# A hybrid decoder layer on one core: marking norm, attention, eviction and residual chains as going ahead in the queues

## The chip, the cores and the metric

One core of one Trainium2 chip runs the whole layer in one launch. The metric is device time in microseconds, from runs of the compiled kernel; the median of three is given, and one more execution is profiled.

## The reference, cut to what matters

Sequence 256, width 2048, all float32. A conditioning vector c gives shift, scale and gate of both halves of the layer.

```
mod = silu(c) @ w_ada + b_ada
sh1, sc1, g1, sh2, sc2, g2 = split(mod, 6)
h = rmsnorm(x, norm1_g) * (1 + sc1) + sh1
q_sb, k_sb, v_sb, q_ds, k_ds, v_ds, q_ix, k_ix, w_ix = split(h @ w_in)
# 8 heads of 128
o_sb = stick_breaking_attention(q_sb, k_sb, v_sb)
# rotary on q_ds, k_ds, q_ix, k_ix; an indexer picks 64 keys per query; 8 heads share k, v
o_ds = dsa_attention(q_ds, k_ds, v_ds, q_ix, k_ix, w_ix * idx_scale)
merged = concat(rmsnorm(o_sb, sb_norm_g), rmsnorm(o_ds, dsa_norm_g))
x = x + g1 * (merged @ w_out)
h2 = rmsnorm(x, norm2_g) * (1 + sc2) + sh2
# up to 2 x 5504, causal depthwise convolution of width 3, silu gate, down
x = x + g2 * conv_ffn(h2, w_up, conv_w, conv_b, w_down)
return rmsnorm(x, final_norm_g)
```

## The kernel before, in words

Activations lie transposed (features on partitions, 256 tokens along the row). Every weight is loaded as 1 MB into one of four `raw` buffers by SP's queue (`load`, L135). `split` (L142) makes a high part with a cast on ACT (`wh`) and the remainder with a subtraction on DVE (`wl`), 1024 columns at a time, four buffers of each. A float32 product is then three matmuls: high by high, low by high, high by low (`nat`, `trn`, `fold`).

The stages, in the order in which they are written:

- The input projection in two parts of eight row blocks each (`do_A`, `do_A2`, `do_V`, `do_QK`); `put` (L346) evicts an accumulator, the second time adding to what is there.
- The sparse-attention group (L518 to L660) for the second part's results: rotary (`rope`), indexer scores `rel`, eight rounds of a maximum per query on DVE, a softmax attention per half of the tokens, and its norm: `rms_b` with the name `rds`, then `norm_o(od)`, which gives `odh` and `odl`. It is written ahead of `do_V` and `do_QK` of the second part (L698 to L701), which PE can do beside it.
- Eight stick-breaking heads, each `do_QK(h)` and then `sb_head(h)`: score `z`, four steps on ACT and one on DVE, a matmul `u` for the running sums, an exponential, the product `o`, and a sum of squares into `sqs` (a part of `ws`; L696).
- The output projection. It has eight blocks m, each with a first half for the sparse heads, `do_O(m, 0)`, and a second half for the stick-breaking heads, `do_O(m, 1)`. Four accumulators exist, so four first halves (L718 to L721) can run before any second half. Behind these in the text stand `rms_b([sqs])` with the name `rsb` (L724) and `norm_o(os_)` (L727), which gives `osh` and `osl`; then the second halves, each followed by `resid` for two of the sixteen row blocks.
- The second norm (`r2`, L762), `modulate` for the feed-forward input (`h2_make`), the up projection with convolution and gate (`do_U`, L835 on), the down projection (L871 on) and the last norm.

The conditioning products are spread over all of this: `ada(j)` (L223) loads 1 MB of `w_ada` and makes one column of `mod` with one DVE product (`wa`, L225); `ada_pe` (L194) makes four on PE (`ap`, `aq`). `pump()` writes a few of them at each call, as many as the string `PLAN` says.

What sets the order in the queues: each instruction gets a number in the order in which it is written. Before the run, a planner goes through the program with a model of the engines. Whenever an engine is free in that model, it queues there the ready instruction with the lowest number. An instruction is ready when its inputs are done and a buffer for its output is free. On the chip each engine then follows its queue in that order. `order(...)` adds single constraints by hand, among others for the first splits of the up projection (L807 to L810).

Of the kernel before, what the change touches and what calls it, by code (L numbers as in the profile page):

```python
# [54 lines left out]
def layer(ctx: ExitStack, tc: tile.TileContext, a, out):  # L55
# [12 lines left out]
    def sm(n, name):  # L68
        return wp.tile([P, n], F32, name=name, tag="sm", bufs=8)

    psum_pool = [None]

    def ps(name, dt=F32, tag="ps"):
# [32 lines left out]
    def rb(name):  # L106
        return wp.tile([P, S], F32, name=name, tag="rb", bufs=2)

    def rms_b(sqs_, width, y, name, tag):


        pt = ps(name + "p", tag=tag)
        for t in range(NT):
            for i, sq in enumerate(sqs_):
                T.matmul(pt[:, t:t + 1], lhsT=sq[:, t * P:(t + 1) * P], rhs=nones[:, 0:1], start=i == 0,
                         stop=i == len(sqs_) - 1)
        nss = pt[:, 0:NT]
        l = sm(NT, name + "l")
        A.activation(l, nss, AF.Ln, scale=-1.0 / width, bias=epsc)
        v = sm(NT, name + "v")  # L120
        V.tensor_scalar(out=v, in0=nss, scalar1=-1.0 / width, scalar2=EPS, op0=ALU.mult, op1=ALU.add)
        r = sm(NT, name + "y")
        A.activation(r, l, AF.Exp, scale=-0.5)
        V.scalar_tensor_tensor(out=l, in0=r, scalar=-0.5, in1=r, op0=ALU.mult, op1=ALU.mult)
        V.tensor_tensor(out=l, in0=l, in1=v, op=ALU.mult)
        last = V.scalar_tensor_tensor(out=r, in0=l, scalar=1.5, in1=r, op0=ALU.add, op1=ALU.mult)
        pt = ps(name + "b", tag=tag)
        for t in range(NT):
            T.transpose(pt[:, t * P:(t + 1) * P], r[:, t:t + 1].to_broadcast([P, P]), ident)
        if y is None:  # L130
            return pt[:, 0:S]
        A.copy(out=y, in_=pt[:, 0:S])
        return last, pt[:, 0:S]
# [145 lines left out]
    for g in range(4):  # L279
        pt = ps(f"cb{g}")  # L280
        for j in range(4):
            k = 4 * g + j
# [9 lines left out]
    V.scalar_tensor_tensor(out=b1, in0=par[:, PB + 16:PB + 32], scalar=1.0, in1=par[:, PN1:PN1 + KT], op0=ALU.add,  # L292
                           op1=ALU.mult)

    def rope(x, t, H, rd, o, name):

        h = rd // 2
        u = s2([P, H, rd], F32, name + "u")
        v = s2([P, H, rd], F32, name + "v")
        c = rc[:, t:t + 1, o:o + rd].to_broadcast([P, H, rd])  # L300
        V.tensor_tensor(out=u, in0=x, in1=c, op=ALU.mult)
        s0 = rs[:, t:t + 1, o:o + h].to_broadcast([P, H, h])
        s1 = rs[:, t:t + 1, o + h:o + rd].to_broadcast([P, H, h])
        V.tensor_tensor(out=v[:, :, 0:h], in0=x[:, :, h:rd], in1=s0, op=ALU.mult)
        V.tensor_tensor(out=v[:, :, h:rd], in0=x[:, :, 0:h], in1=s1, op=ALU.mult)
        V.tensor_tensor(out=x, in0=u, in1=v, op=ALU.add)
# [36 lines left out]
    vsb = b8([P, NT, 1024], F32, "vsb")  # L343
    qk = [b8([P, 8, S], F32, f"qk{i}") for i in range(2)]

    def put(half, dst, src, scale=1.0):  # L346
        if half == 0:
            if scale == 1.0:
                A.copy(out=dst, in_=src)
            else:  # L350
                A.mul(out=dst, in_=src, mul=scale)
        elif scale == 1.0:
            V.tensor_tensor(out=dst, in0=src, in1=dst, op=ALU.add)
        else:
            V.scalar_tensor_tensor(out=dst, in0=src, scalar=scale, in1=dst, op0=ALU.mult, op1=ALU.add)
# [159 lines left out]
    ptag[0] = "acc"  # L515


    for t in range(NT):  # L518
        rope(a2[:, t, 0:ID].rearrange("p (h d) -> p h d", h=1)[:, :, 0:16], t, 1, 16, 32, f"ki{t}")
        rope(qix[:, t, :].rearrange("p (h d) -> p h d", d=ID)[:, :, 0:16], t, IH, 16, 32, f"qi{t}")  # L520
# [15 lines left out]
            A.copy(out=qixT[:, 4 * g:4 * g + 4, t * P:(t + 1) * P], in_=pt.rearrange("p (k t) -> p k t", k=4))  # L536

    sc_n = [0]
    pump()

    def sc_t(L, name):
        sc_n[0] += 1
# [3 lines left out]
    for t in range(NT):  # L546
        L = P * (t + 1)
        cmt = cm[:, P:S] if t == 0 else cm
        npb = 512 // L
        sacc = [None, None]  # L550
        for g in range(8 // npb):
            pts = [ps(f"rel{t}{g}{par_}", tag="att") for par_ in range(2)]
            for j in range(npb):
                for par_ in range(2):
                    T.matmul(pts[par_][:, j * L:(j + 1) * L],  # L555
                             lhsT=qixT[par_ * ID:(par_ + 1) * ID, g * npb + j, t * P:(t + 1) * P],
                             rhs=kixT[par_ * ID:(par_ + 1) * ID, 0:L], start=True, stop=True)
            for par_ in range(2):
                rl = s2([P, npb, L], F32, f"rl{t}{g}{par_}")
                A.activation(rl, pts[par_].rearrange("p (n l) -> p n l", n=npb), AF.Relu)  # L560
                for j in range(npb):
                    h = (g * npb + j) * 2 + par_
                    if sacc[par_] is None:
                        sacc[par_] = sc_t(L, f"sacc{t}{par_}")
                        if par_ == 0:
                            V.scalar_tensor_tensor(out=sacc[0], in0=rl[:, j, :], scalar=wix[:, t, h:h + 1], in1=cmt,
                                                   op0=ALU.mult, op1=ALU.add)
                        else:
                            V.tensor_scalar(out=sacc[1], in0=rl[:, j, :], scalar1=wix[:, t, h:h + 1], scalar2=None,
                                            op0=ALU.mult)  # L570
                    else:
                        V.scalar_tensor_tensor(out=sacc[par_], in0=rl[:, j, :], scalar=wix[:, t, h:h + 1],
                                               in1=sacc[par_], op0=ALU.mult, op1=ALU.add)
        V.tensor_tensor(out=sacc[0], in0=sacc[0], in1=sacc[1], op=ALU.add)
        cur, nxt = sacc
        for r in range(8):
            m8 = sm(8, f"m8{t}{r}")
            V.max(out=m8, in_=cur)
            V.match_replace(out=nxt, in_to_replace=m8, in_values=cur, imm_value=-3e38)
            cur, nxt = nxt, cur  # L580
        mb[t] = scw[:, 6 + t, 0:L // 2].bitcast(BF16)
        V.tensor_scalar(out=mb[t], in0=cur, scalar1=-2e38, scalar2=NEG, op0=ALU.is_gt, op1=ALU.mult)
        V.tensor_tensor(out=mb[t], in0=mb[t], in1=cmt, op=ALU.add)
        pump()

    for t in range(NT):
        rope(a2[:, t, 80:80 + HD].rearrange("p (h d) -> p h d", h=1)[:, :, 0:32], t, 1, 32, 0, f"kx{t}")
# [15 lines left out]
    for t in range(NT):  # L603
# [29 lines left out]
        for g in range(2):  # L633
            pt = ps(f"av{t}{g}", tag="att")
            pv = pt.rearrange("p (k t) -> p k t", k=4)
            for s_ in range(t + 1):
                T.matmul(pv, lhsT=a2[:, s_, 80 + HD:80 + 2 * HD], rhs=pT[:, s_, 4 * g:4 * g + 4, :],
                         start=s_ == 0, stop=s_ == t)
            A.activation(dsq[:, 4 * g:4 * g + 4, t * P:(t + 1) * P], pv, AF.Square)
            for j in range(4):  # L640
                h = 4 * g + j
                A.activation(od[:, h, t * P:(t + 1) * P], pv[:, j, :], AF.Copy, scale=par[:, PDG + h:PDG + h + 1])
        pump()
    for w_ in (4, 2):
        V.tensor_tensor(out=dsq[:, 0:w_, :], in0=dsq[:, 0:w_, :], in1=dsq[:, w_:2 * w_, :], op=ALU.add)
    rdb = rb("rds")
# [1 line left out]
    odh = b8([P, NH, S], F32R, "odh")  # L648
    odl = b8([P, NH, S], F32R, "odl")

    def norm_o(o, rb_, oh, ol):
        for h in range(0, NH, 4):
            sl = slice(h, h + 4)
            V.tensor_tensor(out=o[:, sl, :], in0=o[:, sl, :],
                            in1=rb_.rearrange("p (n t) -> p n t", n=1).to_broadcast([P, 4, S]), op=ALU.mult)
            A.copy(out=oh[:, sl, :], in_=o[:, sl, :])
            V.tensor_tensor(out=ol[:, sl, :], in0=o[:, sl, :], in1=oh[:, sl, :].bitcast(F32), op=ALU.subtract)

    norm_o(od, rdb, odh, odl)
    pump()  # L660


    os_ = b8([P, NH, S], F32, "os")
    sbt = b8([P, D], F32, "sbt")

    def sb_head(h):
        q = qk[h // 4][:, (h % 4) * 2, :]
        k = qk[h // 4][:, (h % 4) * 2 + 1, :]
# [62 lines left out]
    x1T = [b8([P, 8, S], F32, f"x1T{i}") for i in range(2)]  # L731
    sq2 = ws[:, 1536:1792]

    def resid(dst, acc, gate, res, sqsum, k, name):

        resid_i[0] = V.scalar_tensor_tensor(out=dst, in0=acc, scalar=gate, in1=res, op0=ALU.mult, op1=ALU.add)  # L736
        if k == 0:
            A.activation(sqsum, dst, AF.Square)
            return None
        sq = s2([P, S], F32, f"{name}{k}")  # L740
        resid_i[1] = A.activation(sq, dst, AF.Square)  # L741
        if k >= KT - 2:
            return sq
        V.tensor_tensor(out=sqsum, in0=sqsum, in1=sq, op=ALU.add)

    for m in range(8):
# [6 lines left out]
        for p_ in range(2):  # L753
            k = 2 * m + p_
# [13 lines left out]
    def h2_make(k):  # L768
        if k in made:
# [4 lines left out]
        i, j = k // 8, k % 8  # L774
        am = amul[:, 16 + k:17 + k]
        sh = mod_cols(k, 64, 48, am, PN2, b2)
        modulate(h2[k // 4][:, k % 4, 0, :], h2[k // 4][:, k % 4, 1, :], x1T[i][:, j, :], am, r2p if k < 3 else r2, sh,
                 f"g2_{k}", False)

    for k in range(8):  # L780
# [187 lines left out]
```

## Time and profile before

| | us |
|---|---|
| median of 3 runs | 1222.13 (1219.72 to 1223.40) |
| the profiled execution | 1222.48 |
| its span, first to last instruction | 1220.70 |
| PE busy in it | 1154.4 (95%) |
| DVE busy | 879.5 (72%) |
| ACT busy | 632.2 (52%) |
| mean granted TensorE clock | 0.976 |
| read from HBM | 300.24 MB |

PE is TensorE's matmuls, PEld its weight loads, DVE is VectorE, ACT ScalarE, SP the engine that issues the loads. A busy PE isn't PE at its peak: its matmuls overlap, so the distance from one start to the next tells the pace. In a row of the timeline the bracket at the end is the idle time of the engine before that instruction and what ended it; "x4" means that four in a row were merged. A granted clock of 1.00 is 2.4 GHz and 0.50 is 1.2 GHz.

### The profile page before, as it was taken

How to read it: one execution, taken by the hardware profiler on the slowest of the kernel's cores; microseconds unless marked ns; L12 is line 12 of the kernel's file. 1: busy time of each engine (PE TensorE's matmuls, PEld its weight loads, DVE VectorE, ACT ScalarE, POOL GpSimd, SP SyncE). 2: the span in 40 equal slices, each digit the busy share in tenths (PEclk: the TensorE clock that was granted, in tenths of full speed). 3: DMA queues.
4: the chain of work that ended last, by engine and by line, in shares of the span. 5: the costliest groups of instructions: out<-in, count | busy, mean ns of one | idle time of the engine just before them, and what ended most of it. 6: DMA issues, size and time to landing. Idle time of an engine off the chain costs nothing.

```text
span 1220.7 us, 17725 instructions
## 1 busy us (share of the span) xinstructions
PE 1154.4 (95%) x7120; PEld 1018.6 (83%) x7120; DVE 879.5 (72%) x1267; ACT 632.2 (52%) x1004; POOL 0.2 (0%) x4
## 2 busy tenths in 40 slices
PE   3699999899999797999999999999999999999996
PEld 2578997668878797999888888888888888888885
DVE  4877787689766698878789787787876745454543
ACT  3356554457465344456565556555655644444441
POOL 0000000000000000000000000000000000000000
PEclk9799999899999898999999999999999999999998
DMA  8988899668788498776568666675665555555541
GB/s 308 391 318 333 330 324 335 256 222 329 260 341 331 141 346 306 246 275 238 177 246 336 241 210 225 222 254 208 246 224 202 178 198 183 196 184 189 191 139 69
DMA packets 43282, 303.48 MB, mean 249 GB/s; under 512 B 4928, under 2 KB 5440, under 8 KB 7232
## 3 DMA queue, kind: packets, MB, share of 16 engines
q1 hardware_dynamic: 43200, 302.35, 68.1%
q8 instruction: 55, 0.90, 0.3%
q14 instruction: 27, 0.22, 0.0%
HBM read 300.24 MB, written 2.10 MB: 248 GB/s over the span
## 4 chain that ended last, share of the span: by engine, by line
PE 89%; DVE 6%; ACT 3%; DMA 1%; issue 1%; SPq 0%; DVEq 0%; ACTq 0%
PE U L168 21%; PE W L168 13%; PE U L166 11%; PE W L166 7%; PE U L173 3%; PE U L174 3%; PE U L175 3%; PE O L174 3%; PE O L175 3%; PE QK L173 3%; PE QK L175 3%; PE O L173 3%; PE QK L174 3%; DVE wa L225 2%; PE ap L202 1%; PE A L151 1%
## 5 line engine op out<-in xcount | busy, mean ns | idle before, releaser
L225 DVE SCALAR_TENSOR_TENSOR wa<-wa,scb 128x2048 f32<-128x2048 f32 x76 | 173.2, 2284 | 3.8 <-DMA wa<-wa 3.5
L844 ACT COPY u<-U 128x256 f32<-128x256 f32 x70 | 26.1, 372 | 116.6 <-PE U L168 116.6
L845 DVE TENSOR_TENSOR u<-U,u 128x256 f32<-128x256 f32 x70 | 29.3, 420 | 58.7 <-ACT u L844 58.7
L855 DVE SCALAR_TENSOR_TENSOR uc<-u,par,uc 128x255 f32<-128x255 f32 (+1 forms) x140 | 63.8, 478 | 0.8
L851 ACT ACTIVATE uc<-u,par 128x256 f32<-128x256 f32 x70 | 41.9, 601 | 0.0
L862 ACT CAST aT<-uc 128x256 fp32r<-128x256 f32 x43 | 17.4, 404 | 33.3 <-DVE uc L861 33.3
L323 ACT ACTIVATE amul<-mod,b,par 128x1 f32<-128x1 f32 x32 | 12.1, 385 | 42.8 <-DVE wa L225 42.6
L890 DVE SCALAR_TENSOR_TENSOR x1T<-W,mod,x1T 128x256 f32<-128x256 f32 x16 | 7.7, 481 | 31.1 <-PE W L166 31.1
L741 ACT ACTIVATE x2q<-x1T 128x256 f32<-128x256 f32 x15 | 6.3, 418 | 39.1 <-DVE x1T L736 39.0
L326 ACT ACTIVATE mod<-mod,par 128x1 f32<-128x1 f32 x32 | 8.5, 294 | 30.5 <-DVE wa L225 29.4
L202 PE MATMUL ap<-wg,csil 128*32 128x512 f32 x160 | 23.5, 642 | 0.7 <-DMA wg<-wg 0.5
L857 ACT ACTIVATE uc<-uc 128x256 f32<-128x256 f32 x43 | 17.9, 416 | 7.7 <-DVE uc L855 7.6
L861 DVE TENSOR_TENSOR uc<-uc 128x256 f32<-128x256 f32 x43 | 18.2, 422 | 2.8
L863 DVE TENSOR_TENSOR aT<-uc,aT 128x256 fp32r<-128x256 f32 x43 | 18.0, 418 | 0.8 <-ACT aT L862 0.7
L855 DVE SCALAR_TENSOR_TENSOR uc<-U,par,uc 128x255 f32<-128x255 f32 (+1 forms) x32 | 15.0, 478 | 1.0 <-ACT uc L851 0.6
L686 ACT ACTIVATE sbt<-sbt 128x384 f32<-128x384 f32 x8 | 4.2, 525 | 20.6 <-DVE sbt L685 20.6
L202 PEld LDWEIGHTS ap<-wg,csil 128*32 128x32 f32 x160 | 4.3, 115 | 9.4 <-issue 7.0
L736 DVE SCALAR_TENSOR_TENSOR x1T<-O,mod,xT 128x256 f32<-128x256 f32 x16 | 7.0, 479 | 6.7 <-PE O L175 6.7
L555 PE MATMUL rel<-ws,qixT 64*128 64x128 f32 (+1 forms) x64 | 9.8, 390 | 1.5 <-ACT rl L560 1.5
L207 ACT COPY rw<-ap 128x512 f32<-128x512 f32 x5 | 2.9, 581 | 15.5 <-PE ap L202 15.5
L283 PE MATMUL cb<-ident,csil 128*128 128x128 f32 x16 | 3.6, 423 | 7.6 <-DMA ident<-ident 7.6
L151 PE MATMUL A<-wA00h,hh 128*128 128x512 f32 x4 | 2.5, 669 | 8.5 <-ACT hh L318 8.5
(2810 smaller groups left out, 4042.8 us busy)
## 6 DMA issues: line engine op xcount, KB each, us to landing
wU<-wU SPq DMA_DIRECT2D x86, 1024.0 KB, 4.8
wa<-wa SPq DMA_DIRECT2D x76, 1024.0 KB, 6.3
wD<-wD SPq DMA_DIRECT2D x43, 1024.0 KB, 4.8
wg<-wg SPq DMA_DIRECT2D x20, 1024.0 KB, 7.1
wA<-wA SPq DMA_DIRECT2D x16, 1024.0 KB, 6.7
wQK<-wQK SPq DMA_DIRECT2D x16, 1024.0 KB, 6.1
wO<-wO SPq DMA_DIRECT2D x16, 1024.0 KB, 5.7
xT<-xT SPq DMA_DIRECT2D x4, 512.0 KB, 6.0
```

The source lines that it names most:

```text
L166: T.matmul(pt[:, 1, :], lhsT=wl, rhs=x[:, 0, :], start=False, stop=stop)
L168: T.matmul(pt, lhsT=wh, rhs=x, start=first, stop=stop)
L173: T.matmul(pt, lhsT=wh, rhs=xh, start=first, stop=False)
L174: T.matmul(pt, lhsT=wh, rhs=xl, start=False, stop=False)
L175: T.matmul(pt, lhsT=wl, rhs=xh, start=False, stop=last)
L202: T.matmul(pt[32 * j:32 * j + 32, :], lhsT=csil[:, k:k + 1].to_broadcast([P, 32]), rhs=w[:, j * 512:(j + 1) * 512], start=q == 0, stop=q == 3)
L225: i = V.scalar_tensor_tensor(out=w, in0=w, scalar=1.0, in1=scb, op0=ALU.mult, op1=ALU.mult, accum_out=mod[:, j:j + 1])
L844: A.copy(out=u[:, gv, :], in_=acc[gv][:, 1, :])
L845: V.tensor_tensor(out=u[:, gv, :], in0=acc[gv][:, 0, :], in1=u[:, gv, :], op=ALU.add)
L851: A.activation(uc[:, gv, :], u[:, gv, :], AF.Identity, scale=par[:, PCW + 3 * i + 2:PCW + 3 * i + 3], bias=par[:, PCB + i:PCB + i + 1])
L855: V.scalar_tensor_tensor(out=uc[:, gv, sft:S], in0=u[:, gv, 0:S - sft], scalar=par[:, o:o + 1], in1=uc[:, gv, sft:S], op0=ALU.mult, op1=AL ...
L861: V.tensor_tensor(out=uc[:, 1, :], in0=uc[:, 0, :], in1=uc[:, 1, :], op=ALU.mult)
```

## The change

`tc.high_priority()` sets the number of what is written inside it back to the start of the program: the first instruction inside has number 0, the next 1. When it ends, the count goes on from where it had been. The change puts this around a set of chains, so their instructions have lower numbers than any other work that is ready at that moment. Each marked function, and each marked section, starts from 0 again, so marked chains stand among themselves by the place within their own function or section.

A decorator `ahead` marks whole functions: `rms_b` (all norms), `rope`, `put`, `sb_head`, `norm_o`, `resid`, and `modulate` where the second norm's result is applied. `begin()` and `end()` mark the sparse-attention group, left out around each `pump()`, so the conditioning products keep their numbers. Loads, splits and the projections' matmuls keep theirs too. No instruction is added or removed.

```
+    def ahead(f):
+
+        def g(*args, **kw):
+            with tc.high_priority():
+                return f(*args, **kw)
+        return g
+
+    guard = []
+
+    def begin():
+        guard.append(tc.high_priority())
+        guard[-1].__enter__()
+
+    def end():
+        guard.pop().__exit__(None, None, None)
...
+    @ahead
     def rms_b(sqs_, width, y, name, tag):
...
+    @ahead
     def rope(x, t, H, rd, o, name):
...
+    @ahead
     def put(half, dst, src, scale=1.0):
...
+    begin()
     for t in range(NT):
         rope(a2[:, t, 0:ID].rearrange("p (h d) -> p h d", h=1)[:, :, 0:16], t, 1, 16, 32, f"ki{t}")
...
     sc_n = [0]
+    end()
     pump()
+    begin()
...
         V.tensor_tensor(out=mb[t], in0=mb[t], in1=cmt, op=ALU.add)
+        end()
         pump()
+        begin()
...
                 A.activation(od[:, h, t * P:(t + 1) * P], pv[:, j, :], AF.Copy, scale=par[:, PDG + h:PDG + h + 1])
+        end()
         pump()
+        begin()
...
+    @ahead
     def norm_o(o, rb_, oh, ol):
...
     norm_o(od, rdb, odh, odl)
+    end()
     pump()
+    begin()
+    end()
...
+    @ahead
     def sb_head(h):
...
+    @ahead
     def resid(dst, acc, gate, res, sqsum, k, name):
...
-        modulate(h2[k // 4][:, k % 4, 0, :], h2[k // 4][:, k % 4, 1, :], x1T[i][:, j, :], am, r2p if k < 3 else r2, sh,
+        ahead(modulate)(h2[k // 4][:, k % 4, 0, :], h2[k // 4][:, k % 4, 1, :], x1T[i][:, j, :], am, r2p if k < 3 else r2, sh,
                  f"g2_{k}", False)
```

## Rows read from the trace of the kernel before

**Rows 1.** The page: the span, and each engine's busy time, share and instructions.

```profile
span 1220.7 us, 17725 instructions
PE 1154.4 (95%) x7120; PEld 1018.6 (83%) x7120; DVE 879.5 (72%) x1267; ACT 632.2 (52%) x1004; POOL 0.2 (0%) x4
```

**Rows 2.** Busy time by stretch; columns in the first row.

```profile
core 0: us, PE busy (x) PEld busy (x) DVE busy (x) ACT busy (x) POOL busy (x), PEclk, DMA share, GB/s
225.00:300.00 75.00, 70.28 (x397) 52.24 (x396) 66.28 (x162) 48.82 (x121) 0.00 (x0) 0.93 0.68 255
300.00:394.50 94.50, 91.13 (x675) 78.55 (x674) 66.25 (x87) 51.26 (x94) 0.00 (x0) 1.00 0.83 316
500.00:1200.00 700.00, 700.00 (x4239) 629.10 (x4238) 490.69 (x673) 374.89 (x533) 0.00 (x0) 1.00 0.61 215
...
375.00:394.70 19.70, 19.47 (x159) 19.15 (x159) 12.54 (x15) 10.31 (x18) 0.00 (x0) 1.00 0.94 359
394.70:412.00 17.30, 9.31 (x55) 8.53 (x55) 9.81 (x12) 5.24 (x8) 0.00 (x0) 0.70 0.34 134
412.00:475.00 63.00, 63.00 (x527) 63.00 (x527) 51.62 (x63) 29.43 (x43) 0.00 (x0) 1.00 0.81 299
...
398.20:408.40 10.20, 5.40 (x22) 4.71 (x23) 6.11 (x9) 2.85 (x4) 0.00 (x0) 0.50 0.50 202
```

**Rows 3.** Timeline of PE around the `rsb` norm: start, duration, instruction, idle before.

```profile
394.50 0.50 PE L115 MATMUL rsbp<-nones,ws 128*128 128x1 f32 x4
399.74 0.69 PE L129 MATMUL rsbb<-ident,rsby 128*128 128x128 f32 x2 [4.73 <-DVE rsby L126]
403.22 0.58 PE L173 MATMUL O<-osh,wO010h 128*128 128x256 f32 x1 [2.80 <-ACT osh L656]
...
411.84 0.28 PE L175 MATMUL O<-osh,wO011l 128*128 128x256 f32 x1
411.96 0.28 PE L174 MATMUL O<-osl,wO110h 128*128 128x256 f32 x1
```

**Rows 4.** Timeline of DVE in the same stretch.

```profile
382.16 0.42 DVE L696 TENSOR_TENSOR ws<-ws,sbt 128x256 f32<-128x256 f32 x1
384.14 1.23 DVE L146 TENSOR_TENSOR wO301l<-wO,wO301h 128x1024 fp32r<-128x1024 f32 x1 [1.56 <-ACT wO301h L145]
...
396.93 2.28 DVE L225 SCALAR_TENSOR_TENSOR wa<-wa,scb 128x2048 f32<-128x2048 f32 x1
```

**Rows 5.** Timeline of DVE and ACT around the twin norm, `rds`.

```profile
296.85 0.68 DVE L645 TENSOR_TENSOR dsq<-dsq 128x512 f32<-128x512 f32 x1
...
305.10 2.19 ACT L656 CAST odh<-od 128x1024 fp32r<-128x1024 f32 x2 [1.28 <-DVE od L654]
...
307.26 2.35 DVE L657 TENSOR_TENSOR odl<-od,odh 128x1024 fp32r<-128x1024 f32 x2
```

**Rows 6.** Timeline of ACT and DVE at the second norm, `r2`.

```profile
478.09 1.03 ACT L145 CAST wU101h<-wU 128x1024 fp32r<-128x1024 f32 x1
479.02 0.20 ACT L123 ACTIVATE r2y<-r2l 128x2 f32<-128x2 f32 x1
...
480.76 2.28 DVE L225 SCALAR_TENSOR_TENSOR wa<-wa,scb 128x2048 f32<-128x2048 f32 x1
```

**Rows 7.** Timeline of PE where the last head follows the one before.

```profile
371.35 0.38 PE L689 MATMUL o<-sbt,vsb 128*128 128x128 f32 x2
371.57 0.33 PE L671 MATMUL z<-sbm,identb 128*128 128x384 bf16 x1
```

**Rows 8.** Groups of DVE from 297 to 385: busy us, mean ns, idle before.

```profile
L225 DVE SCALAR_TENSOR_TENSOR wa<-wa,scb 128x2048 f32<-128x2048 f32 x8 | 18.3, 2282 | 0.4 <-DMA wa<-wa 0.4
L685 DVE TENSOR_TENSOR sbt<-u,sbt 128x384 f32<-128x384 f32 x8 | 4.4, 554 | 5.7 <-PE u L683 5.7
L680 DVE SCALAR_TENSOR_TENSOR sbt<-z,sbt 128x384 f32<-128x384 f32 x8 | 4.4, 553 | 4.6 <-ACT sbt L679 4.6
```

**Rows 9.** Waits of SP's queue: us in total, times, longest.

```profile
SPq L137 <- DVE wa L225: 155.5, 53, 7.3
```

## The prediction

> **What bounds the kernel now.** I read the page's busy shares first, then the stretches, then the order of time around each hole of PE. PE is busy for 1154.4 of 1220.7 us [rows 1]. From 500 to 1200 it is busy for 700.00 of 700.00 us at full clock [rows 2], so nothing that only reorders DVE or ACT there can gain, and the whole feed-forward part moves as one block behind whatever comes before it. The holes lie earlier. From 225 to 300 PE is idle for 4.7 us, from 300 to 394.5 for 3.4 us, and from 394.7 to 412 for 8.0 of 17.3 us, with a mean clock of 0.70 [rows 2]. That last stretch is the largest hole behind the start, and what ends it is one chain: the norm of the stick-breaking heads (`rsb`).
>
> The reader should see three times. The sum of squares that this norm needs is complete at 382.16 + 0.42 = 382.58 us [rows 4]. Its first matmul, `rsbp`, runs on PE only at 394.50 [rows 3], 11.9 us later, although its data are there. In between PE runs first halves of the output projection (`do_O(m, 0)` of L719), which are written ahead of L724 and therefore have the lower number. Then PE has nothing left that doesn't need `osh`, and it waits: 4.73 us for `rsbb`, 2.80 us for `osh` [rows 3]. The chain is in the wrong place by its number, not by its data.
>
> **The change part by part.** No instruction is added or removed; numbers are changed. I go by which other ready work a marked instruction overtakes: only work that is written earlier, since later work is already behind it.
>
> *The `rsb` norm and `norm_o(os_)`.* These overtake `do_O(0..3, 0)` and the `wa` products of L225 that are pumped before them. So `rsbp` goes to about 382.7 us, and its chain runs beside what is left of the first halves. Does it fit? The twin of this chain, `rds` with `norm_o(od)`, is written ahead of the projections that run beside it, so it shows what such a chain takes when nothing written earlier than it holds it up: its sum is complete at 296.85 + 0.68 = 297.53 us, its first `odh` cast begins at 305.10 (7.6 us later), its last `odl` ends at 307.26 + 2.35 = 309.61 (12.1 us later), with splits for the next weights among its steps [rows 5]. Put on 382.58 that gives `osh` from 390.2 and the last `osl` at 394.7, against 394.5 at which PE runs out of first halves today, plus about 1.2 us of `rsbp` and `rsbb` that now lie before that point (0.50 and 0.69) [rows 3]. It fits, narrowly, and the last `osl` isn't needed by the first matmuls. DVE has room: 12.54 us of 19.7 are busy from 375 to 394.7 [rows 2], and the chain brings two pairs of 2.4 us like the twin's and small change, some 5.5 us. A `wa` of 2.28 us that then comes later has no reader on this path.
>
> What that is worth: from 394.50 to 411.96 us PE does the 48 matmuls of `do_O(0, 1)`, one more, and the norm's own. At full clock one follows the other in 0.12 us [rows 3], so 49 are 5.9 us; with 1.2 us for the norm's it is 7.1 instead of 17.46 us. The gain is 10.4 us. Of this 7.5 us are the two waits; the other 2.9 are the third, short wait and matmuls at half clock: the granted clock is 0.50 (1.2 GHz) from 398.2 to 408.4 [rows 2], after PE had stood nearly still from 394.7, and without the hole I expect no fall.
>
> The Trainium skill (TensorE: Matmul & The Clock Gate, Terms) prices throttled time at its length times one less the granted share: 10.2 us at 0.50 would be 5.1 us on top of the waits, a time of about 1209.5. Half of this slow stretch is itself waiting, which a faster clock doesn't shorten, so the row decides. Nothing below rests on this paragraph.
>
> Can the rest follow 10.4 us earlier? From 394.7 to 475 the DMA engines bring 134 x 17.3 + 299 x 63 = 21.2 MB (GB/s times us, in thousandths); in 69.9 us that is 303 GB/s, and 359 is shown just before [rows 2]. DVE does 9.8 + 51.6 = 61.4 us in 80.3 us there; less the 5.5 that move ahead, 56 in 69.9. Both fit, so I carry the gain through whole.
>
> *The heads (`sb_head`, and `put` of their q and k).* These overtake `wa` and the PE form of it. Eight `wa` of 2.28 us stand among the heads' steps from 297 to 385 [rows 8]. But one head still follows the other: each `z` comes on PE directly behind the `o` of the head before (371.35, then 371.57) [rows 7], which I read as tiles of one kind being given out in written order, and a mark doesn't alter that. PE is busy for 91.13 of 94.5 us meanwhile [rows 2], so the gain is between 0 and 3.4 us. The loss is between 0 and 18.8 us, worked out under the third rival. I take 0: these heads are covered by projections, and PE's idle time there is already small.
>
> *The sparse-attention group (L518 to L660).* It is written ahead of the last value and query projections that fill PE, so it overtakes `wa`, `ap` and some of its own later parts, whose numbers now start again at each section. The gain is at most the 4.7 us of idle PE from 225 to 300; for the loss I set the same once more, as an estimate, because DVE is busy for 66.3 of 75 us there [rows 2] and any other order of its work is an order of the same work. I take 0.
>
> *The second norm (`r2`) and `modulate`.* Here the mark changes little. `r2y` of L123 is written before the weights of `do_U(1, 0)`, and yet the cast `wU101h` (478.09) goes ahead of it (479.02) [rows 6]. So the planner fills an idle engine with what is ready and doesn't hold it for a step that is about to be; a better number doesn't prevent that, nor the `wa` at 480.76 while `r2b` is on PE. Between 0 and 3.3 us (the 1.03 us cast and the 2.28 us `wa`) could be gained; I take 0. `resid` and the later `modulate` sit beside a full PE, and the first and last norms have little beside them: 0 both ways.
>
> **Sum.** The profiled execution took 1222.48 us (span 1220.70), 0.35 above the median of 1222.13. 1222.48 - 10.4 = 1212.1, so a median of 1211.7 us. With the terms taken as 0 but small, its own range is 1207 to 1216.
>
> **The rivals.**
> *Half hidden.* The chain starts early but is stretched: two `wa` of 2.28 us put in where a step isn't ready yet, as at 396.93 today [rows 4], make the twin's 12.1 into 16.7 us, to 399.3. `do_O(0, 1)` then waits some 4.2 us behind its start at 395.1, and perhaps 1 us goes to a clock that falls: 1222.1 - 5.2 = 1216.9. For it: the planner fills gaps [rows 6]. Against: the twin met the same fillers.
>
> *No move.* The planner's own clock could have the sum ready only when the first halves are out, and then the mark changes nothing: 1222.1. Against it: on DVE the split `wO301l` (384.14), part of the last first half, is queued behind the sum [rows 4], so the plan had the sum ready while first halves were still to come.
>
> *Slower: held buffers.* The weight buffers that the `wa` products share with all loads come free only when the product is done, and SP's queue, which issues every load in order, already waits for `wa` 155.5 us in 53 waits [rows 9]. Where a `wa` comes behind the DVE steps of a head (0.55, 0.55 and 0.42 us, and two evictions of q and k that I take at 0.42 each: 2.35 in all) [rows 4, 8] its buffer and the next load are late by that. Eight of them make 18.8 us if each reaches PE. It turns into a loss when more than 10.4 of 18.8, 55%, arrives; at 85% the time is 1222.1 - 10.4 + 16 = 1228. For it: 359 GB/s from 375 to 394.7 leaves little room to catch up. Against: PE's small idle time from 300 to 394.5 says that loads run ahead.
>
> **How the numbers follow.** Forecast 0.58 (1211.7), half hidden 0.17 (1216.9), no move 0.08 (1222.1), held buffers 0.17 (1228). A measurement of this kernel can tell 0.3%, 3.7 us, from no change: faster is below 1218.5. Faster: 0.58 and two thirds of the half-hidden case, 0.69. Same: the rest of that case and no move, 0.14. Slower: 0.17. For 8 in 10 the range goes from 1205 (the forecast with the heads' 3.4 and part of the other small gains) to 1228.
>
> **What would show it.** Right: `rsbp` on PE within a microsecond or two of the last `ws` sum, among `do_O(m, 0)`; the waits of 4.73 and 2.80 us gone; no fall of the clock there; the feed-forward block of the same length, only earlier. Wrong: `rsbp` still behind `do_O(3, 0)`; or PE waiting for `osl` or for splits in the second halves; or new PE idle time from 225 to 394 with SP waiting longer on `wa`.

## The result, and the profile after

The change makes the kernel slower: 1229.71 us (1225.99 to 1230.93, 5 runs) against 1221.47 (1218.17 to 1223.4, 5 runs), a ratio of 1.0067 with a 95% interval of 1.0043 to 1.0091. That is 8.2 us more where 10.4 less was forecast, and outside the range. The profiled execution of the change took 1225.99 us, the shortest of its five, so its trace holds about 4 of the 8.2 us.

The page after, its first lines, for [rows 1]:

```profile
span 1224.2 us, 17725 instructions
...
PE 1156.5 (94%) x7120; PEld 1018.5 (83%) x7120; DVE 881.1 (72%) x1267; ACT 630.8 (52%) x1004; POOL 0.2 (0%) x4
```

Busy time by stretch after, for [rows 2]; columns in the first row:

```profile
core 0: us, PE busy (x) PEld busy (x) DVE busy (x) ACT busy (x) POOL busy (x), PEclk, DMA share, GB/s
225.00:264.00 39.00, 35.83 (x207) 24.93 (x208) 33.88 (x102) 22.11 (x41) 0.00 (x0) 1.00 0.65 237
264.00:294.00 30.00, 23.89 (x159) 21.89 (x158) 29.46 (x51) 7.91 (x18) 0.00 (x0) 0.90 0.94 355
294.00:300.00 6.00, 6.00 (x41) 5.13 (x40) 2.14 (x3) 5.40 (x19) 0.00 (x0) 0.94 0.45 175
300.00:394.50 94.50, 90.99 (x618) 72.92 (x617) 65.65 (x91) 60.49 (x137) 0.00 (x0) 1.00 0.75 286
...
500.00:1200.00 700.00, 700.00 (x4247) 629.37 (x4246) 493.55 (x677) 375.31 (x535) 0.00 (x0) 1.00 0.60 217
```

The work is the same and the feed-forward block is as long as before. New is the second row, which read like this before:

```profile
264.00:294.00 30.00, 30.00 (x156) 23.33 (x155) 27.55 (x34) 23.84 (x73) 0.00 (x0) 0.98 0.76 280
```

After, PE stands idle for 6.1 of these 30 us at a mean clock of 0.90, ACT works for 7.91 us where it had 23.84, and DVE is busy for 29.46. So DVE is the place to look. In that stretch it runs the top-k rounds of the sparse-attention group: eight pairs of MAX8 and MATCH_REPLACE8 for each half of the tokens, each step needing the one before. One round of the second half, first before (the line numbers of the change are 17 to 32 higher), then after:

```profile
254.16 0.41 DVE L578 MAX8 m<-scw 128x8 f32<-128x256 f32 x1
254.50 0.40 DVE L306 TENSOR_TENSOR qds<-qx0u,qx0v 128x256 f32<-128x256 f32 x1
...
254.90 0.41 DVE L579 MATCH_REPLACE8 scw<-m,scw 128x256 f32<-128x256 f32 x1
255.22 0.18 DVE L301 TENSOR_TENSOR kx1u<-ws,scw 128x32 f32<-128x32 f32 x1
...
255.41 0.42 DVE L578 MAX8 m<-scw 128x8 f32<-128x256 f32 x1
```

```profile
282.95 0.43 DVE L600 MAX8 m<-scw 128x8 f32<-128x256 f32 x1
283.29 2.28 DVE L242 SCALAR_TENSOR_TENSOR wa<-wa,scb 128x2048 f32<-128x2048 f32 x1
...
286.22 0.41 DVE L601 MATCH_REPLACE8 scw<-m,scw 128x256 f32<-128x256 f32 x1
286.55 2.28 DVE L242 SCALAR_TENSOR_TENSOR wa<-wa,scb 128x2048 f32<-128x2048 f32 x1
...
288.76 0.43 DVE L600 MAX8 m<-scw 128x8 f32<-128x256 f32 x1
```

Before, short pieces of the same group (rope, 0.18 to 0.40 us) lie between the steps and a round takes 1.25 us. After, a `wa` of 2.28 us lies behind each step and the round takes 5.8; it is the longest, and the mean from one MAX8 to the next is 3.7 us in this half (1.4 before). Between the first MAX8 of the second half (262.7 us) and its last (288.8) there are six `wa` and four splits of 1.22 us, 18.6 of the 26.0 us; before, one split in 9.9 us. The marked rope and scores start again at a low number, so they ran ahead of the rounds; then only long work was left to put between them.

The second half is not the whole delay. The last MAX8 is 30.4 us later than before. Of this, 6.2 lie ahead of the first round (239.65 before, 245.82 after): the scores of the second half now stand in front of it. Another 8.0 lie in the rounds of the first half (8.7 us before, 16.7 after, with one `wa` and four splits among them), and 16.2 in those of the second.

What the late group does to its neighbours is in the next views. First SP's queue, which issues every load in order:

```profile
262.62 0.33 SPq L154 DMA_DIRECT2D wQK<-wQK  x1
269.00 8.59 SPq L154 DMA_DIRECT2D wa<-wa  x4
279.80 0.33 SPq L154 DMA_DIRECT2D wQK<-wQK  x1
```

What it waited for most from 255 to 300 us (us in total, times, longest):

```profile
SPq L154 <- DVE m L600: 20.2, 5, 6.4
```

Then ACT's cast of the weights of that load, and PE's first products with them:

```profile
286.49 1.04 ACT L162 CAST wQK1200h<-wQK 128x1024 fp32r<-128x1024 f32 x1 [12.15 <-DMA wQK<-wQK]
```

```profile
287.58 0.38 PE L190 MATMUL QK<-hh,wQK1200h 128*128 128x256 f32 x1 [2.88 <-ACT wQK1200h L162]
...
291.35 0.58 PE L192 MATMUL QK<-hh,wQK1200l 128*128 128x256 f32 x1 [3.23 <-DVE wQK1200l L163]
```

SP waits 20.2 us for DVE's position at the rounds (before, no wait of SP in that stretch is put down to them), the load behind goes out at 279.80, and ACT stands idle for 12.15 us until it lands. But this load isn't late. All of SP's waits for DVE from 255 to 300 us come to 31.4 us, and to 41.6 before; and before, the same cast runs 9.5 us later:

```profile
295.94 1.07 ACT L145 CAST wQK1200h<-wQK 128x1024 fp32r<-128x1024 f32 x1
```

It is PE that is early. It comes to these weights at 287.58, before at 301.84, because it had used its other work: the projections that lie beside the group's softmax before were done while the group was stuck. So PE waits 2.88 and 3.23 us, and the granted clock is 0.50 from 287.9 to 294.7.

Last the norm that the prediction was about, on DVE [rows 4] and on PE [rows 3]:

```profile
396.92 0.42 DVE L727 TENSOR_TENSOR ws<-ws,sbt 128x256 f32<-128x256 f32 x1
397.26 2.28 DVE L242 SCALAR_TENSOR_TENSOR wa<-wa,scb 128x2048 f32<-128x2048 f32 x1
```

```profile
397.53 0.53 PE L132 MATMUL rsbp<-nones,ws 128*128 128x1 f32 x4
...
401.36 0.28 PE L192 MATMUL O<-odh,wO301l 128*128 128x256 f32 x1
401.50 0.43 PE L146 MATMUL rsbb<-ident,rsby 128*128 128x128 f32 x2
406.12 0.58 PE L190 MATMUL O<-osh,wO010h 128*128 128x256 f32 x1 [4.19 <-ACT osh L683]
```

`rsbp` does follow the sum at once, 0.2 us behind it. But the sum itself now comes at 397.34, not at 382.58, and four us later the first halves are used up. The chain is exposed again and the clock falls again (0.50 from 404.0 to 410.8).

### The profile page after: what moved, and what is told of

The parts are those of the page before. It is cut to its first block, busy times and chain, and to the rows that moved or that the text cites. A ratio compares the mean times of both kernels' runs of the same rounds, so it can differ in the third digit from the quotient of the medians.

```text
span 1224.2 us, 17725 instructions
## 1 busy us (share of the span) xinstructions
PE 1156.5 (94%) x7120; PEld 1018.5 (83%) x7120; DVE 881.1 (72%) x1267; ACT 630.8 (52%) x1004; POOL 0.2 (0%) x4
## 4 chain that ended last, share of the span: by engine, by line
PE 87%; DVE 8%; ACT 2%; DMA 2%; issue 1%; SPq 0%; DVEq 0%; ACTq 0%
PE U L185 21%; PE W L185 13%; PE U L183 11%; PE W L183 7%; DVE wa L242 3%; PE U L190 3%; PE O L191 3%; PE U L191 3%; PE U L192 3%; PE O L190 3%; PE O L192 3%; PE QK L192 2%; PE QK L190 2%; PE QK L191 2%; PE A L168 2%; PE A L169 2%
## 5 line engine op out<-in xcount | busy, mean ns | idle before, releaser
L922 DVE SCALAR_TENSOR_TENSOR x1T<-W,mod,x1T 128x256 f32<-128x256 f32 x16 | 7.7, 482 | 31.7 <-PE W L183 31.7
L219 PE MATMUL ap<-wg,csil 128*32 128x512 f32 x160 | 26.5, 675 | 0.5 <-PE aq L227 0.5
L344 ACT ACTIVATE mod<-mod,par 128x1 f32<-128x1 f32 x32 | 8.4, 290 | 30.4 <-DVE wa L242 28.3
L889 ACT ACTIVATE uc<-uc 128x256 f32<-128x256 f32 x43 | 17.9, 415 | 8.0 <-DVE uc L887 7.9
L883 ACT ACTIVATE uc<-U,par 128x256 f32<-128x256 f32 x16 | 9.0, 562 | 2.3 <-DVE uc L887 2.3
L577 PEld LDWEIGHTS rel<-ws,qixT 64*128 64x128 f32 x64 | 7.1, 186 | 3.6 <-ACT rl L582 3.1
```

Of the source, the lines that this page charges most:

```text
L219: T.matmul(pt[32 * j:32 * j + 32, :], lhsT=csil[:, k:k + 1].to_broadcast([P, 32]), rhs=w[:, j * 512:(j + 1) * 512], start=q == 0, stop=q == 3)
L883: A.activation(uc[:, gv, :], u[:, gv, :], AF.Identity, scale=par[:, PCW + 3 * i + 2:PCW + 3 * i + 3], bias=par[:, PCB + i:PCB + i + 1])
```

## The experiments

All were run in 4 to 12 timed executions against the kernel before (medians of 1220.73 to 1221.0 us in each set), the change once more in two single executions. Starts are those of the profiled execution, which need not be a median one: that of e9 is the longest of its five (1220.2 us), that of e12 the shortest of its twelve (1215.6). In us: the last MAX8 of the group; its norm's `rdsp`; the sum of squares of the heads complete; `rsbp`; the last matmul of the first halves; the first of the second halves; the first U product (up projection).

| kernel | MAX8 | rdsp | sum | rsbp | last first half | first second half | U | median us |
|---|---|---|---|---|---|---|---|---|
| before | 258.4 | 298.1 | 382.6 | 394.5 | 394.4 | 403.2 | 484.4 | 1221.5 |
| the change | 288.8 | 323.4 | 397.3 | 397.5 | 401.4 | 406.1 | 487.4 | 1229.7 |
| e1 | 258.5 | 295.0 | 379.4 | 380.0 | 391.8 | 391.9 | 470.2 | 1208.8 |
| e2 | 282.6 | 320.8 | 389.9 | 397.5 | 397.4 | 404.5 | 485.9 | 1224.3 |
| e3 | 260.2 | 305.7 | 385.5 | 386.1 | 393.4 | 395.6 | 477.2 | 1215.7 |
| e4 | 259.0 | 296.9 | 381.3 | 381.9 | 393.7 | 393.8 | 472.5 | 1210.6 |
| e6 | 274.4 | 309.2 | 388.9 | 396.5 | 396.4 | 403.5 | 484.9 | 1222.0 |
| e9 | 262.8 | 308.4 | 393.2 | 393.3 | 397.9 | 400.2 | 482.3 | 1216.3 |
| e10 | 258.7 | 296.6 | 371.3 | 371.8 | 393.9 | 394.0 | 472.3 | 1209.4 |
| e11 | 257.8 | 297.1 | 371.8 | 372.3 | 394.4 | 394.5 | 473.1 | 1211.8 |
| e12 | 277.2 | 311.8 | 390.1 | 390.2 | 398.1 | 398.3 | 477.8 | 1220.3 |

**e1: the step that the forecast priced, alone.** To the kernel before:

```diff
-    rms_b([sqs], NH * HD, rsb, "rsb", "att")
+    ahead(rms_b)([sqs], NH * HD, rsb, "rsb", "att")
...
-    norm_o(os_, rsb, osh, osl)
+    ahead(norm_o)(os_, rsb, osh, osl)
```

> The kernel before with one place marked: rms_b of rsb and norm_o(os_). Theory A (the loss comes from the marks in the sparse group, whose renumbered parts push the top-k rounds apart, and the mark on rsb is worth what was forecast): 10 us under before, 8 to 11, with rsbp before 385 us. Theory B (held weight buffers: marked chains put wa back and loads come late): the same gain, since no head is marked. Theory C (the hole is filled but loads or splits then run out, so the gain is given back before the second norm): within 3 us of before.

Measured 1208.84 us, ratio 0.9902 [0.9884, 0.992]. The norm now runs in the middle of the first halves:

```profile
379.91 0.28 PE L181 MATMUL O<-odl,wO200h 128*128 128x256 f32 x1
380.03 0.50 PE L122 MATMUL rsbp<-nones,ws 128*128 128x1 f32 x4
380.39 0.36 PE L182 MATMUL O<-odh,wO200l 128*128 128x256 f32 x1
...
383.10 0.38 PE L136 MATMUL rsbb<-ident,rsby 128*128 128x128 f32 x2
```

The second halves follow the first without a wait, at full clock. This step is worth some 12 us, and the loss comes from elsewhere.

**e2: the sparse-attention group alone**, with its rope, norm and `norm_o`; every section starts again from 0 as in the change. Without the marks on the rest:

```diff
-    @ahead
     def put(half, dst, src, scale=1.0):
...
-    @ahead
     def sb_head(h):
...
-    @ahead
     def resid(dst, acc, gate, res, sqsum, k, name):
```

> The kernel before with only the sparse group marked, its sections and functions counting from 0 as in the change; heads, rsb, put, resid and modulate unmarked. Theory A: slower than before by 4 to 9 us, the last top-k round ends 15 us or more later than 261 us, and rdsp runs after 310 us. Theory B: within 3 us of before, since no head is ahead of wa.

1224.34 us, ratio 1.003 [1.0018, 1.0041]: 3.6 us slower, a little under what was expected. The rounds end 24 us late, as expected, yet most of that is absorbed: the kernel before had its sum ready 11.9 us ahead of `rsbp` and could lose that for nothing.

**e3: the change without the group** (no `begin`/`end`, no mark on rope).

```diff
-    begin()
...
-    end()
...
-    @ahead
     def rope(x, t, H, rd, o, name):
```

> The change without its marks on the sparse group and on rope; all other functions marked, each counting from 0. Theory A: top-k ends near 261 us as before, and most of the rsb gain is there: 5 to 10 us under before. Theory B: no better than the change, 4 to 9 us over before, because the heads are still ahead of wa.

1215.69 us, ratio 0.9958 [0.9942, 0.9974]: 14.0 us under the change, so the group costs that much once the rest is marked; but still 6.9 over e1, with `rdsp` 10.7 us later than there.

**e4: all of the change's marks, one running count**: marked work goes ahead of unmarked, in written order among itself.

```diff
     def ahead(f):
...
         def g(*args, **kw):
-            with tc.high_priority():
-                return f(*args, **kw)
+            if guard:
+                return f(*args, **kw)
+            begin()
+            r = f(*args, **kw)
+            end()
+            return r
...
-        guard.append(tc.high_priority())
+        guard.append(tc.high_priority(offset=tc.cur_priority - count[0]))
         guard[-1].__enter__()
...
     def end():
+        count[0] = tc.cur_priority
         guard.pop().__exit__(None, None, None)
```

> All that the change marks is marked, but the marked work has one running count in written order, so it is ahead of everything else and keeps its own order. Theory A: top-k ends near 261 us, 8 to 11 us under before. Theory B: slower than before by 4 to 9 us, as the change. Theory C: within 3 us of before.

1210.61 us, ratio 0.9917 [0.9901, 0.9933]. The same marks without the restarts cost 1.8 us over e1, and the intervals overlap. What hurts is the order that restarting makes among the marked steps, not that they go ahead of the rest.

**e6: the group with its sections counted on; rope, the norm and `norm_o` start from 0.**

To e2:

```diff
-        guard.append(tc.high_priority())
+        guard.append(tc.high_priority(offset=tc.cur_priority - count[0]))
...
     def end():
+        count[0] = tc.cur_priority
```

> The sparse-attention group alone, its sections counted on from one another as they were written, and only rope, the rds norm and norm_o starting again from number 0. The group's work then has its old order among itself, but for the ropes, which no longer stand between the top-k rounds of the second token half. Gap theory (the rounds wait for long stripe operations because the short work that used to lie between them was used up earlier): the planned DVE queue has six splits and two wa between the first and the last round of the second half, so that half takes 14 to 22 us (before 9.9, the change 26.1), rdsp starts 305 to 318 us, and the run is 1220 to 1226. Rival, that the sections' restarts are needed for the loss: last round within 3 us of 258, rdsp within 3 of 298, time within 2 us of before.

The "stripe operations" of this text are `wa` and the splits. 1221.97 us, ratio 1.0014 [1.0004, 1.0023]. The second half's rounds take 20.1 us (before 9.9), with two `wa` and six splits among them, although only the ropes were pulled out from between them. The mechanism shows; its price without the marked `rsb` norm is about 1 us.

**e9 and e10: which mark makes e3 slower than e1.** Each is e1 with one mark more.

```diff
+    @ahead
     def put(half, dst, src, scale=1.0):
```

> The rsb norm marked as in e1, and put (the evictions and sums of A, A2, V and QK) marked as well, nothing else. It asks which mark makes e3 some 7 us slower than e1. If put: its sums start again from 0 and go ahead of the group's steps, rdsp starts 303 to 308 us as in e3 (e1: 295.0), and the time is 1213 to 1217. If it is the heads' marks (the second o product behind the next head's z): this run stays within 2 us of e1, 1207 to 1211, with rdsp within 2 us of 295.

```diff
+    @ahead
     def sb_head(h):
```

> The rsb norm marked as in e1, and the standard-attention heads (sb_head) marked as well, nothing else. If put is what makes e3 slower: rdsp within 2 us of 295, the sum of the heads' squares complete at or before e1's 379.4, and the time 1205 to 1210. If the heads' marks are: PE's queue has the next head's z between the two o products of a head, which wait for each other's buffers, and the time is 1212 to 1217.

e9 took 1216.26 us, ratio 0.9962 [0.9949, 0.9975]; e10 took 1209.44, ratio 0.9912 [0.9899, 0.9925]. So it is `put`, and the heads' mark, which brings the sum 8 us forward, neither gains nor costs. In e9 the group is stretched ahead of its last row maximum: this comes 24.2 us behind the last MAX8 in e1 and 31.7 in e9. The last row maximum and the sum of the group's squares on DVE, in e1 and then in e9:

```profile
282.77 0.67 DVE L624 TENSOR_REDUCE nm<-lg 128x2 f32<-128x512 f32 x1
...
292.32 1.22 DVE L652 TENSOR_TENSOR dsq<-dsq 128x1024 f32<-128x1024 f32 x1
```

```profile
294.48 0.67 DVE L625 TENSOR_REDUCE nm<-lg 128x2 f32<-128x512 f32 x1
...
305.16 1.21 DVE L653 TENSOR_TENSOR dsq<-dsq 128x1024 f32<-128x1024 f32 x1
```

Seven splits of QK weights lie on DVE between the last MAX8 and `dsq`, in e1 four. That the sums of `put` bring the projections forward at the group's cost fits this, but no run isolates it.

**e11: the change without the group's marks and without `put`'s.** e3 with

```diff
-    @ahead
     def put(half, dst, src, scale=1.0):
```

> The change without two of its marks: the sparse-attention group (with rope) and put are left as they were; rms_b, norm_o, sb_head, resid and the ff modulates stay marked. If the group and put are the whole of the loss, this is as fast as e1 and e10: 1206 to 1211, rsbp beside the first O halves at 371 to 381 us, and the time behind 480 us as before. If resid, the modulates or the other norms cost or gain, it differs from e10 (1209.4) by more than 2 us, and by the start of the first U product against e10's 472.3 one sees whether that happens before or behind it.

1211.81 us, ratio 0.9925 [0.9911, 0.9938], just above the range expected. It is 2.4 us over e10, a little more than the 2 us that the expectation set for a cost of the remaining marks (`resid`, the modulates, the other norms). The intervals overlap and the first U product is only 0.8 us later, so such a cost is neither shown nor excluded. The two marks taken out are 17.9 of the 20.9 us between e1 and the change.

**e12: the whole change, with the short work held back** so that it can lie between the rounds again; no mark and no number altered:

```diff
-            V.max(out=m8, in_=cur)
+            i = V.max(out=m8, in_=cur)
+            if r == 0:
+                round1 = i
...
+                        if t == 1:
+                            order(i, round1)
...
+        if o == 0:
+            order(i, round1)
```

> The whole change, all marks and restarts kept, with one thing added: the second half's scores may run only after the first round of the first half, and the ropes of kx and qx only after the first round of the second half, so that short work is there again to lie between rounds. Gap theory: the planned DVE queue has three wa and three splits between the first and last round of the second half (the change: six wa, four splits; before: one split), so the half takes 14 to 20 us (the change 26.1, before 9.9), rdsp starts 305 to 315 us (the change 323.4), and the time lies 3 to 9 us under that of the change, 1220 to 1226. If the loss comes from the marks outside the group or from the restarts themselves: within 2 us of the change's 1229.7.

1220.3 us (1215.6 to 1223.41 in 12), ratio 0.9993 [0.9981, 1.0005]: 9.4 us under the change, slightly more than expected. The second half's rounds take 21.3 us, a little over the 14 to 20 expected, with three `wa` and three splits among them, and the group's norm starts 11.6 us earlier than in the change. Of this, 4.8 us lie in the second half's rounds and 0.8 in the first half's; 6.0 lie ahead of the first round, which the held-back scores no longer precede. `put` is still marked in it. So the order of DVE's work in and around the rounds, with every mark kept, takes back all of what the change lost against the kernel before. That is direct evidence for the order; how much of the time belongs to the filled gaps, and how much to the earlier first round, e12 doesn't separate.

**Two more executions of the change.**

> The change itself, unaltered, once more: its profiled execution took 1226.0 us, the other four 1228.9 to 1230.9, so one execution of that kind is still to be seen in a trace. If the spread comes from the stretch where the stripes are late (264 to 325 us), rdsp starts later than 323.4 here by as much as the time is longer; if from the norm's chain behind the first O halves, the stretch 394 to 412 us holds it.

> The same as change_look_2, for a second trace of an execution of the change: the last top-k round between 286 and 292 us and rdsp at or behind 322 in each, if the order of the queue and not chance sets them.

They took 1226.18 and 1227.66 us, with the last round at 288.3 and 289.8 and `rdsp` at 323.5 and 324.4. The sequence is the same each time. Neither was an execution of 1229 to 1231 us, so where those lose 3 to 4 us more is not seen.

## Why the prediction was wrong

*The `rsb` norm: right.* From the first product of O to the last, the kernel before takes 361.1 to 475.1, 114.0 us, and e1 357.9 to 460.9, 103.0: 11.0 us gained where the sum had 10.4. The twin was a good measure, too: in e1 the first `osh` cast begins 8.1 us after the sum and the last `osl` ends 11.5 us after it (7.6 and 12.1 from the twin), 1 us before the second halves begin. The Trainium skill's rule for throttled time (TensorE: Matmul & The Clock Gate, Terms) would have made it 12.6, an estimate (7.5 of waits and 5.1); the trace is nearer to the row than to the rule. The rest of e1's shorter span, 3.2 us, lies ahead of the first O product: the trace of before shows the clock at 0.50 there twice (234.4 to 241.2 and 261.7 to 265.1), that of e1 not at all. This isn't the mark's doing: up to the norm, PE, ACT and DVE run the same instructions in the same order in both traces. The change keeps of this step only its order: without it (e2) the way from the last first half to the first second half is 7.1 us, with it (the change) 4.8, in e1 0.1.

*The sparse-attention group: the step that failed.* It was taken as 0 with a bound of 4.7 us to either side, "because DVE is busy for 66.3 of 75 us there and any other order of its work is an order of the same work". The busy time did stay (66.28 before, 65.47 after from 225 to 300). But the rounds are a chain, and what counts for the group is when its last step runs, not how much work its engine does. A planner that leaves no gap puts a whole `wa` behind a step when nothing shorter is at hand, and scores that start again at a low number go in front of the first step: the chain's end moved by 30 us, and the group with its mark costs 3.6 us alone (e2) and 14.0 beside the other marks (the change against e3), where the term was 0. The rule was in the prediction itself: "the planner fills an idle engine with what is ready and doesn't hold it for a step that is about to be". I used it for `r2` and not for the longest dependent chain on DVE. I also had read that the sections' numbers start again, and didn't ask what the chain's present neighbours were and where they would go.

*The heads and `put`: taken as 0, together.* The heads are 0 (e10 against e1: 0.6 us more, intervals overlapping). `put` costs 7.4 us (e9 against e1), inside the bound of 18.8, but by another way than the bound's.

*`r2`, `modulate`, the rest: 0,* as taken, within what e11 can tell (2.4 us over e10).

*Why the terms don't add.* On the kernel before the group costs 3.6 us, on top of e3 14.0. The `rsb` norm's old place left 11.9 us of slack behind the heads' sum, and a late group used it up unseen. The first step of the change turns this slack into time, and then each us by which the sum is late counts. Between e1 and the change the first U product moves by 17.2 us: the first halves end 9.5 later, the wait behind them is 4.6 longer, and 3.0 come after it, with a clock of 0.94 against 0.97. Of the 9.5, PE's idle time from 225 us on makes 4.4 (12.8 against 8.4); the rest lies in longer busy time, partly at half clock.

*The rivals.* "Held buffers" gave 1228, near the time, but by luck, for a wrong reason: SP's queue waits for `wa` 153.7 us in 52 waits against 155.5 in 53 [rows 9], and e4, with every mark, isn't slower. "Half hidden" is what the end of the change's chain looks like (one `wa` at 397.26 behind the sum and ahead of `rsbv`), but as a result of the late group. Its price holds a small slip: the second halves were put at 395.1, but with all of the norm's 1.2 us on PE they begin at 395.7, which makes 1216.3 instead of 1216.9 and changes no chance. "No move" is refuted by `rsbp`, 0.2 us behind its sum.

## What to carry to other kernels

Moving a chain ahead pays where its data are ready and the engine that will wait still has other work: mark that chain alone (here 11.9 us for two calls). Before marking a serial chain's neighbours, list what lies between its dependent steps today and what will lie there once that is gone; where an engine is never left idle by the planner, each step can come behind the longest ready operation. Marks that each restart their numbers reorder the marked work among itself; one running count keeps the old order and came within 1.8 us of the best version here. That best version is e1, faster than both kernels.

## What the runs showed of the hardware

Dependent steps on DVE need no filler between them. Where nothing was put between two steps after the change, MATCH_REPLACE8 and the MAX8 that reads its result stood like this:

```profile
258.94 0.29 DVE L600 MAX8 m<-scw 128x8 f32<-128x128 f32 x1
...
259.34 0.28 DVE L601 MATCH_REPLACE8 scw<-m,scw 128x128 f32<-128x128 f32 x1
259.65 0.29 DVE L600 MAX8 m<-scw 128x8 f32<-128x128 f32 x1
```

The last line begins 0.03 us after the one above it ends (0.04 at twice the width, in e6); an independent operation behind MAX8 begins 0.09 us before that ends (283.29 against 282.95 + 0.43). So a dependence costs about 0.1 us here, and the whole round took 0.71 us with nothing between its steps. Each gap into which 2.28 us of `wa` were put was worth no more than that 0.1 us.
